# Hybrid decoder block on one core: the hi and lo halves of q and k carried across the partitions by DMAs instead of by 64-row copies, with a scheduler that models drains

## The chip, the cores and the metric

The kernel runs on one core of one Trainium2 chip. The metric is the device time of one execution in microseconds (us). The kernel before takes 1377.05 us (median of 3 runs, 1376.73 to 1377.36). TensorE (PE) does matrix products, VectorE (DVE) and ScalarE (ACT) do elementwise work, GpSimd (POOL) clears a few buffers, and SyncE (SP) issues every DMA from one queue, in the order in which the program lists them. Each engine works through its own list in order; between engines, semaphores make an instruction wait for what it reads, and for the buffer that it overwrites.

## What is computed

The reference is a decoder trunk of two layers over one sequence of 512 tokens, model width 1024, in float32. Cut to what matters here, a layer is:

```
h = rmsnorm(x, norm_g);  proj = h @ w_in
# branch A: differential attention, 8 heads, 2 maps of 64
q = rope(rmsnorm(aq)); k = rope(rmsnorm(ak))
a = softmax(causal(q0 k0^T)) - lam * softmax(causal(q1 k1^T))
oa = rmsnorm(a @ av) * silu(az);  ya = oa @ w_out_a
# branch B: mLSTM matrix memory, 8 heads, q and k of 64 columns
mq, mk = split(silu(causal_conv(bqk)))
hb = rmsnorm(mlstm(mq, mk, bv, bi, bf)) * sigmoid(bo) * silu(bz);  yb = hb @ w_out_b
u = sigmoid(ga) * ya + sigmoid(gb) * yb
x = x + u @ w_o
```

## The kernel before, in words

**Precision in two halves.** Matrix products run in float32r, a reduced form of float32. To keep accuracy, an operand is kept as two tiles: hi, the value cast to float32r (an ACT copy), and lo, the rest (a DVE subtraction); `split` at line 453 records the pair. A product of two such operands is three matmuls: hi by hi, hi by lo, lo by hi (`mm3`, line 457). So each weight piece of 128x1024 is loaded into one of two raw buffers (`wr`), cast into `wh`, and subtracted into `wl`; `wh` and `wl` have three buffers each. With `wsp` set, the subtraction is done in two halves of 128x512 (line 1388).

**Pieces.** A layer is 104 weight pieces and a small one for the gates. The order of the named groups stands in `TUNE["order"]`: `qk0` are the four pieces that make q and k of heads 0 and 1 (chunk c = 0 of 4), `av` the values, `az`, `ga`, `gb`, `bo`, `bz` the gates, `bqk` q and k of branch B, `woa`, `wob`, `wo` the output products.

**q and k of branch A.** When a chunk's product for 128 tokens (tt = 0 to 3) is complete, `qk_done` (line 744) makes the squares for the norm and the rotary turn. Then `back` (line 809) lets PE transpose four 128x128 blocks into one PSUM tile `qkt`. That tile comes from a pool with a single buffer (tag `tr`), which also serves `ut` (the transposed attention weights), `msp`, `den`, `gft` and others, so the next of these can't start until the last reader of the previous one is done. In `qkt`, rows 0 to 63 hold map 0 and rows 64 to 127 map 1. The score product of each map wants q as hi in one 64-row half and lo in the other, and k as hi in both. So `back` reads `qkt` ten times in pieces of 64x256: six ACT copies (q hi, k hi twice, for each map) and four DVE subtractions (q lo, k lo, for each map), half of them crossing from one half of the partitions to the other. There are 32 such backs in a run: 2 layers, 4 chunks, 4 blocks of tokens.

**q and k of branch B.** `bqk_done` (line 917) does the same after the convolution: for each of 8 pieces in a layer, ACT copies and DVE subtractions of 64x512 out of the tile `cv`.

**The order of the work.** Engines' lists are not written by hand. All operations are first recorded with their dependences (`Recorder.add`, line 159), then `schedule` (line 252) plays them through a model of five engines: at each step the engine that can start first takes, of what is ready, the operation with the least key (a due time worked back from the matmul that needs it). SP takes the earliest recorded. The costs, latencies and due times in `TUNE` set the order; the chip then runs the lists as they are, and waits where the model was wrong.

**Tiles named below.** `s2` is a ring of seven 128x512 buffers for short-lived tiles. Tiles `qk_0x` and `qk_2x`, or `qs` and `ks`, hold q and k of a chunk for the score products `sc`; `kl` holds k lo. `mq`, `mql` and `mk` are their like in branch B. `dd` and `em` are decay tables of branch B, read by DMAs from a DRAM tile `rows`.

Of the kernel before, what the change touches and what calls it, by code (L numbers as in the profile page):

```python
# [9 lines left out]
F32 = mybir.dt.float32  # L10
# [27 lines left out]
    "order": (  # L38
# [4 lines left out]
    ),  # L43
    "qkt": 4,
    "gct": 14,
    "gls": 6,
    "glf": 10,
    "attn": (1, 5, 5, 9, 9, 10, 13, 16, 16, 19, 24),
    "a0": 23,
    "ap": 18,  # L50
    "a4": 6,
    "ml": (0, 10, 11, 12, 16, 28),
    "ahead": 3,
    "lc": 2,
    "slack": 3400.0,
    "margin": 200.0,
    "pemargin": 0.0,
    "wait": 300.0,
    "swpen": 6000.0,
    "smargin": 135.0,  # L60
    "pwait": 7.0,
    "wdiff": 8000.0,
    "wsp": 1,
    "kact": (0, 1, 2),
    "qsq": (1, 3),
    "foldA": (0, 2, 3, 4, 5, 6, 7),
    "foldM": (0, 1, 2, 3, 4, 5, 6, 7),
    "foldD": (0, 1, 2, 3, 4, 5, 6, 7),
    "warm": 18,
    "start": 'x0 ng w0 x1 ct w1 x2 x3',  # L70
    "gateA": 10,
    "gateM": 4,
    "actp": (0, 3),
    "m0": 221,
    "mp": 14,
    "m4": 10,
    "slots": 20,
}

# [17 lines left out]
class Recorder:  # L97
# [61 lines left out]
    def add(self, eng, e, fn, a, k):  # L159
# [41 lines left out]
        if eng == "PE":  # L201
            self.pe_time += cost
        self.ops.append({"eng": eng, "e": e, "fn": fn, "a": a, "k": k, "pre": preds, "cost": cost, "nom": self.pe_time})

    @staticmethod
    def cost(eng, fn, a, k):
# [25 lines left out]
        if eng == "DVE":  # L232
# [13 lines left out]
            return x  # L246
        return 60.0

# [3 lines left out]
    def schedule(self):  # L252
# [32 lines left out]
        for i in reversed(range(n)):  # L285
            o = ops[i]
            v = o["nom"] if o["eng"] == "PE" else o["nom"] + TUNE["slack"]
# [11 lines left out]
        table = 6  # L299
        order = []  # L300

        def admit(i):
# [11 lines left out]

        todo = [i for i in range(n) if not left[i]]
        while len(order) < n:
            for i in todo:
                ready[ops[i]["eng"]].append(i)
            todo = []
            best = None  # L320
            cand = {}
            for e, r in ready.items():
                c = []
                for i in r:
                    s = admit(i)
                    if s is not None:
                        c.append((s, i))
                if c:
                    cand[e] = c
# [17 lines left out]
            ready[e].remove(i)  # L347
            s = max(s, pick[2])
            load = None
            o = ops[i]  # L350
            c = o["cost"]
            if e == "ACT":
                sets = self.ACT_SET.get(self.func(o))
                if sets and table not in sets:
                    s = max(s, free[e] + 1283.0)
                    table = sets[0]
                    load = table
            free[e] = s + c
            end[i] = s + c
            if e == "SP":  # L360
                size = 4.0
                for x in list(o["a"][0].shape):
                    size *= x
                dma = max(dma, s) + size / 360.0
                end[i] = max(dma, s) + 2000.0
            for t in o["tiles"]:
                r = rings[t["ring"]]
                if not t["live"]:
                    t["live"] = True
                    m = min(r["free"])  # L370
                    r["free"].remove(m)
# [5 lines left out]
                if not t["left"]:  # L377
                    r["free"].append((t["rel"], t["name"]))
            o["load"] = load
            order.append((s, len(order), i))  # L380
# [28 lines left out]
def kernel(ctx, tc, x, pos, wp, wg, cst, par, pb, ngb, out):  # L409
# [181 lines left out]
    def layer_events(l):  # L591
# [208 lines left out]
        def qk_back(c, tt, rq):  # L800
# [8 lines left out]
            def back():  # L809
# [3 lines left out]
                ts = slice(tt * P, (tt + 1) * P)  # L813
                q0, q1, k0, k1 = (t[:, :, ts] for t in st[("qs", c)])
                kl0, kl1 = (t[:, :, ts] for t in st[("kl", c)])
# [101 lines left out]
        def bqk_done(m, acc):  # L917
# [17 lines left out]
            if kind == 0:  # L935
# [432 lines left out]
    def prep(i):  # L1368
# [131 lines left out]
```

## Time and profile before

| | before |
|---|---|
| median of 3 runs | 1377.05 us |
| profiled execution, device time | 1378.8 us |
| its span (first to last instruction) | 1377.0 us |
| PE busy | 1354.3 us (98%) |
| DVE busy | 999.8 us (73%) |
| ACT busy | 883.7 us (64%) |
| DMA queue of SP | 48304 packets, 136.54 MB, 33.0% of 16 engines |

How to read it: busy is time in which an engine has an instruction in flight. Matmuls are pipelined, so the records of two neighbours overlap, and a busy PE may still be short of its full rate. A group's row in the profile names the line, the engine, the operation, the tile written and the tiles read, the shape, the count, the busy time, the mean of one in ns, and the engine's idle time just before them, with what ended it. Every operation of this kernel has the same line (405 before, 429 after), because the recorder issues them all; so tiles tell the operations apart.

### The profile page before, as it was taken

How to read it: one execution, taken by the hardware profiler on the slowest of the kernel's cores; microseconds unless marked ns; L12 is line 12 of the kernel's file. 1: busy time of each engine (PE TensorE's matmuls, PEld its weight loads, DVE VectorE, ACT ScalarE, POOL GpSimd, SP SyncE). 2: the span in 40 equal slices, each digit the busy share in tenths (PEclk: the TensorE clock that was granted, in tenths of full speed). 3: DMA queues.
4: the chain of work that ended last, by engine and by line, in shares of the span. 5: the costliest groups of instructions: out<-in, count | busy, mean ns of one | idle time of the engine just before them, and what ended most of it. 6: DMA issues, size and time to landing. Idle time of an engine off the chain costs nothing.

```text
span 1377.0 us, 17949 instructions
## 1 busy us (share of the span) xinstructions
PE 1354.3 (98%) x6356; PEld 1099.4 (80%) x6356; DVE 999.8 (73%) x1974; ACT 883.7 (64%) x1808; POOL 23.0 (2%) x28
## 2 busy tenths in 40 slices
PE   9999999999999999999999999999999999999999
PEld 7787777888888878888887877878788877888887
DVE  7988988886367868844569889888853777787442
ACT  6868968886246858733366788688752467687230
POOL 1000010000000000000000000000000000000000
PEclk9999999999999999999999999999999999999999
DMA  4222221223334444433512222221333444444332
GB/s 174 92 63 92 62 78 62 77 77 111 95 108 127 119 117 124 131 102 108 189 49 92 63 75 77 78 71 53 116 90 103 108 125 120 117 119 129 104 119 86
DMA packets 48394, 137.68 MB, mean 100 GB/s; under 512 B 5776, under 2 KB 12560, under 8 KB 48304
## 3 DMA queue, kind: packets, MB, share of 16 engines
q1 hardware_dynamic: 48304, 136.54, 33.0%
q8 instruction: 50, 0.82, 0.2%
q14 instruction: 40, 0.33, 0.1%
HBM read 132.25 MB, written 4.26 MB: 99 GB/s over the span
## 4 chain that ended last, share of the span: by engine, by line
PE 63%; DVE 15%; ACT 14%; DMA 5%; issue 2%; SPq 1%; ACTq 0%; DVEq 0%
PE qk L405 10%; PE wo L405 6%; PE wob L405 6%; PE bv L405 6%; PE woa L405 6%; PE gb L405 5%; PE av L405 4%; PE bo L405 4%; DVE wl L405 3%; DMA dd<-rows 3%; PE bz L405 3%; PE ga L405 3%; PE bqk L405 3%; ACT wh L405 2%; ACT p L405 2%
## 5 line engine op out<-in xcount | busy, mean ns | idle before, releaser
L405 DVE TENSOR_TENSOR wl<-wr,wh 128x512 fp32r<-128x512 f32 x400 | 265.7, 686 | 103.9 <-ACT wh L405 100.0
L405 ACT CAST wh<-wr 128x1024 fp32r<-128x1024 f32 (+1 forms) x202 | 210.9, 1044 | 201.7 <-PE woa L405 43.8
L405 PE MATMUL qk<-wh,hh 128*128 128x512 f32 x256 | 99.5, 405 | 0.2 <-ACT hh L405 0.2
L405 PE MATMUL qk<-wh,hl 128*128 128x512 f32 x256 | 99.4, 401 | 0.0
L405 PE MATMUL qk<-wl,hh 128*128 128x512 f32 x256 | 98.9, 402 | 0.1
L405 ACT ACTIVATE p<-sc,mx,rq 128x128 f32<-128x128 f32 (+3 forms) x128 | 78.8, 618 | 12.8 <-DVE mx L405 12.2
L405 PE MATMUL wob<-ob,wh 128*128 128x512 f32 x256 | 84.7, 389 | 0.0
L405 PE MATMUL woa<-oa,wh 128*128 128x512 f32 x256 | 79.9, 389 | 0.0
L404 ACT ACT_TABLE_LOAD x61 | 78.3, 1283 | 1.1
L405 PEld LDWEIGHTS qk<-wl,hh 128*128 128x128 f32 x256 | 48.0, 188 | 11.1 <-DVE wl L405 2.1
L405 PEld LDWEIGHTS wob<-ob,wh 128*128 128x128 f32 x256 | 48.0, 188 | 10.1
L405 PEld LDWEIGHTS woa<-oa,wh 128*128 128x128 f32 x256 | 48.1, 188 | 9.8
L405 PEld LDWEIGHTS qk<-wh,hh 128*128 128x128 f32 x256 | 48.1, 188 | 9.6 <-ACT hh L405 0.5
L405 PEld LDWEIGHTS qk<-wh,hl 128*128 128x128 f32 x256 | 48.1, 188 | 9.1 <-DVE hl L405 0.4
L405 DVE TENSOR_REDUCE mx<-sc 128x2 f32<-128x256 f32 (+1 forms) x64 | 52.5, 820 | 0.7
L405 PE MATMUL az<-hh,wh 128*128 128x512 f32 x128 | 50.5, 402 | 0.0
L405 PE MATMUL bo<-hl,wh 128*128 128x512 f32 x128 | 50.3, 393 | 0.0
L405 PE MATMUL bo<-hh,wh 128*128 128x512 f32 x128 | 50.3, 393 | 0.0
L405 PE MATMUL bo<-hh,wl 128*128 128x512 f32 x128 | 50.3, 393 | 0.0
L405 PE MATMUL az<-hl,wh 128*128 128x512 f32 x128 | 50.2, 400 | 0.0
L405 PE MATMUL az<-hh,wl 128*128 128x512 f32 x128 | 49.3, 395 | 0.0
L405 PE MATMUL bqk<-hh,wl 128*128 128x512 f32 x128 | 48.2, 397 | 0.7 <-DVE wl L405 0.7
(273 smaller groups left out, 3661.4 us busy)
## 6 DMA issues: line engine op xcount, KB each, us to landing
wr<-in_wp_dram SPq DMA_DIRECT2D x208, 512.0 KB, 3.5
dd<-rows SPq DMA_DIRECT2D x16, 256.0 KB, 4.0
em<-rows SPq DMA_DIRECT2D x16, 256.0 KB, 3.4
dd<-rows SPq DMA_DIRECT2D x16, 192.0 KB, 5.1
x<-in_x_dram SPq DMA_DIRECT2D x4, 512.0 KB, 7.4
dd<-rows SPq DMA_DIRECT2D x16, 128.0 KB, 6.2
xr<-in_x_dram SPq DMA_DIRECT2D x8, 256.0 KB, 4.3
x1d<-xn SPq DMA_DIRECT2D x8, 256.0 KB, 3.6
```

The source lines that it names most:

```text
L404: self.tc.keep_in_program_order(self.nc.scalar.preload_act_table_set(self.SET_NAME[o["load"]]))
L405: self.tc.keep_in_program_order(getattr(o["e"], o["fn"])(*o["a"], **o["k"]))
```

## The change

Three things change.

First, `back` and `bqk_done` no longer copy in 64-row pieces. A new helper `halves` takes two `s2` tiles and makes hi and lo of the whole 128x512 tile, one ACT copy and one DVE subtraction. Then DMAs, issued by SP, carry each 64-row half to its places, ten of 64x256 (64 KB) for each back, six or four of 64x512 (128 KB) for each piece of branch B. That is 320 and 80 DMAs more in a run.

Second, the scheduler's model. A DMA's issue costs 400 ns instead of 60, a transfer that doesn't come from the DRAM inputs goes at 175 bytes per ns instead of 360, and an ACT or DVE instruction whose first output or input starts at another partition than that of the instruction before it starts 115 ns later (and is put off by `drain` in the choice). There are also a bias on the due time by the kind of tile, and a penalty for starting late.

Third, the table. The order of pieces and the offsets are new, `ahead` is 5 instead of 3, `wsp` is 0, so that `wl` is one subtraction of 128x1024. Some small choices move: `qsq` and `kact` let ACT do fewer column-wise squares and scalings, `actp` one block more, and `foldM` and `foldD` lose one head each, which adds four matmuls.

```
     "order": (
...
-    "wsp": 1,
-    "kact": (0, 1, 2),
-    "qsq": (1, 3),
+    "wsp": 0,
+    "kact": (0, 1),
+    "qsq": (1,),
...
-        return 60.0
+        return 400.0
...
+                    if e in at_rows and ops[i]["rows"] != at_rows[e]:
+                        k += TUNE["drain"]
+                    if s - q < TUNE["risk"] and e != "SP":
+                        k += TUNE["late"]
...
+            if e in at_rows:
+                if o["rows"] != at_rows[e]:
+                    s = max(s, free[e] + 115.0)
+                at_rows[e] = o["rows"]
...
-                dma = max(dma, s) + size / 360.0
+                src = o["a"][1]
+                dma = max(dma, s) + size / (175.0 if src.space != DRAM or src.tensor.name.startswith("rows") else 360.0)
...
+    def halves(src, name):
+
+        hi, lo = t2(f"h_{name}", F32R), t2(f"l_{name}", F32R)
+        split(hi, lo, src)
+        return hi.bitcast(F32), lo.bitcast(F32)
...
+                h4, l4 = halves(pst.rearrange("p a b -> p (a b)"), f"qk{l}_{c}_{tt}")
+                h4, l4 = (t.rearrange("p (a b) -> p a b", a=4) for t in (h4, l4))
...
                 for q, k, kl, a, b in ((q0, k0, kl0, L, H), (q1, k1, kl1, H, L)):
-                    A.copy(q[a], pst[a, 0:2, :])
-                    V.tensor_tensor(q[b], pst[a, 0:2, :], q[a].bitcast(F32), ALU.subtract)
-                    A.copy(k[a], pst[a, 2:4, :])
-                    A.copy(k[b], pst[a, 2:4, :])
-                    V.tensor_tensor(kl[a], pst[a, 2:4, :], k[a].bitcast(F32), ALU.subtract)
+                    SY.dma_start(q[a], h4[a, 0:2])
+                    SY.dma_start(k[a], h4[a, 2:4])
+                    SY.dma_start(k[b], h4[a, 2:4])
+                    SY.dma_start(q[b], l4[a, 0:2])
+                    SY.dma_start(kl[a], l4[a, 2:4])
...
+            hi, lo = halves(y, f"m{l}_{m}")
...
-                    A.copy(q[a, i, :], y[a])
-                    A.copy(q[b, i, :], y[a])
-                    V.tensor_tensor(st[("mql", grp)][i][a, pl, :], y[a], q[a, i, :].bitcast(F32), ALU.subtract)
+                    SY.dma_start(q[a, i, :].bitcast(F32), hi[a])
+                    SY.dma_start(q[b, i, :].bitcast(F32), hi[a])
+                    SY.dma_start(st[("mql", grp)][i][a, pl, :].bitcast(F32), lo[a])
...
-                    A.copy(k[a, i, :], y[a])
-                    V.tensor_tensor(k[b, i, :], y[a], k[a, i, :].bitcast(F32), ALU.subtract)
+                    SY.dma_start(k[a, i, :].bitcast(F32), hi[a])
+                    SY.dma_start(k[b, i, :].bitcast(F32), lo[a])
...
-        if TUNE["wsp"]:
+        if i < TUNE["wsp"]:
```

How the lists move is shown at two places. The first is DVE's list in layer 0, while the last chunk (c = 3) is turned: tile `qkt0_3_0` is its first block of tokens, `qs` and `kl` the q and k lo of that chunk, `wl30` a weight's lo. Before:

```order
L405 TENSOR_TENSOR qs00_3_497<-qkt0_3_0_533,qs00_3_497 64x2x128
L405 TENSOR_TENSOR rq0_3_503<-qy0_3_1_509,qt0_3_1_510 128x16
L405 TENSOR_TENSOR wl30_489<-wr30_487,wh30_488 128x512 x2
L405 TENSOR_REDUCE qss0_3_2_516<-sq0_3_2_515 128x8
L405 TENSOR_TENSOR rot0_3_2_517<-qk0_3_2_469,ctab0_143 128x512
L405 TENSOR_TENSOR kl00_3_501<-qkt0_3_0_533,ks00_3_499 64x2x128
L405 TENSOR_TENSOR sq0_3_2_515<-qk0_3_2_469,stab0_144 128x8x32 x2
L405 TENSOR_TENSOR qs10_3_498<-qkt0_3_0_533,qs10_3_498 64x2x128
L405 TENSOR_TENSOR rot0_3_2_517<-rot0_3_2_517,sq0_3_2_515 128x512
L405 TENSOR_TENSOR sc0_5_0_529<-sc0_5_0_529,ct_94 128x2x128
L405 TENSOR_TENSOR kl10_3_502<-qkt0_3_0_533,ks10_3_500 64x2x128
```

After, the same place of DVE's list:

```order
L429 TENSOR_TENSOR rot0_3_3_535<-qk0_3_3_488,ctab0_154 128x512
L429 TENSOR_TENSOR l_qk0_3_0_548<-qkt0_3_0_546,h_qk0_3_0_547 128x512
L429 TENSOR_TENSOR sq0_3_3_534<-qk0_3_3_488,stab0_155 128x8x32 x2
L429 SCALAR_TENSOR_TENSOR mx0_4_3_543<-mx0_4_3_543,rq0_2_396 128x2
L429 RECIPROCAL sums0_4_2_524<-sums0_4_2_524 128x2
L429 TENSOR_TENSOR rot0_3_3_535<-rot0_3_3_535,sq0_3_3_534 128x512
L429 TENSOR_TENSOR sums0_4_2_524<-sums0_4_2_524,ml0_158 128x2
L429 TENSOR_TENSOR wl31_500<-wr31_498,wh31_499 128x1024
```

Four reads of the PSUM tile with nine other instructions between them have become one read.

The second place is SP's list in layer 0, around the load of piece 9 (`wr9`, the first of `qk1`). Before, the loads follow each other:

```order
L405 DMA wr5_154<-in_wp_dram 128x1024
L405 DMA wr6_175<-in_wp_dram 128x1024
L405 DMA wr7_185<-in_wp_dram 128x1024
L405 DMA wr8_192<-in_wp_dram 128x1024
L405 DMA wr9_201<-in_wp_dram 128x1024
L405 DMA wr10_211<-in_wp_dram 128x1024
```

After, with the q and k of chunk 0 in `qk0_0x` (`h_qk0_0_3` and `l_qk0_0_3` are the new hi and lo tiles of its last block of tokens):

```order
L429 DMA kl10_0_165<-l_qk0_0_2_195 64x2x128
L429 DMA qk0_0x_163<-h_qk0_0_3_197 64x2x128 x3
L429 DMA qk0_0x_163<-l_qk0_0_3_198 64x2x128
L429 DMA kl00_0_164<-l_qk0_0_3_198 64x2x128
L429 DMA qk0_0x_163<-h_qk0_0_3_197 64x2x128 x3
L429 DMA qk0_0x_163<-l_qk0_0_3_198 64x2x128
L429 DMA kl10_0_165<-l_qk0_0_3_198 64x2x128
L429 DMA wr9_199<-in_wp_dram 128x1024
L429 DMA wr10_206<-in_wp_dram 128x1024
```

These are the last of forty DMAs of chunk 0 that now stand between `wr7` and `wr9`, with `wr8` alone among them. On PE's list the first matmul that reads the weights of `wr9` stands 127 matmuls after the last transpose of `qkt0_0_0`, the block whose halves the forty DMAs begin with: 89 of 512 columns, 4 of 384, 5 of 256 and 29 of 128 or fewer. In layer 1 the load after chunk 0's first twenty is `wr114`, and that after all forty is `wr115`.

More of the change, by code (lines that the diff above doesn't have):

```diff
@@ L45 @@
     "gct": 14,
-    "gls": 6,
-    "glf": 10,
-    "attn": (1, 5, 5, 9, 9, 10, 13, 16, 16, 19, 24),
+    "gls": 7,
+    "glf": 12,
+    "attn": (1, 5, 5, 9, 9, 10, 13, 16, 16, 19, 26),
     "a0": 23,
     "ap": 18,
[L51 to L55, printed above, removed]
-    "margin": 200.0,
[L57 to L62, printed above, removed]
-    "wsp": 1,
-    "kact": (0, 1, 2),
@@ L65 @@
-    "qsq": (1, 3),
+    "a4": 8,
+    "ml": (2, 8, 10, 10, 15, 30),
+    "ahead": 5,
+    "lc": 10,
+    "slack": 11872.4,
+    "margin": 200.0,
+    "pemargin": 560.8,
+    "wait": 223.4,
+    "swpen": 7168.1,
+    "smargin": 15.0,
+    "pwait": 0.5,
+    "wdiff": 2579.7,
+    "wsp": 0,
+    "kact": (0, 1),
+    "qsq": (1,),
     "foldA": (0, 2, 3, 4, 5, 6, 7),
-    "foldM": (0, 1, 2, 3, 4, 5, 6, 7),
-    "foldD": (0, 1, 2, 3, 4, 5, 6, 7),
+    "foldM": (0, 1, 2, 3, 4, 5, 6),
+    "foldD": (0, 1, 2, 3, 4, 5, 7),
@@ L69 @@
     "warm": 18,
     "start": 'x0 ng w0 x1 ct w1 x2 x3',
[L71 to L76, printed above, removed]
+    "gateA": 9,
+    "gateM": 0,
+    "actp": (0, 1, 3),
+    "m0": 226,
+    "mp": 15,
+    "m4": 7,
     "slots": 20,
+    "bias": {'ga': -5500.0, 'sgb': -13300.0, 'den': -10150.0, 'bo': 2250.0, 'qk': -150.0, 'bv': -10450.0, 'gft': 3750.0, 'az': 1250.0, 'bqk': 1600.0, 'ut': 11800.0, 'ht': -10800.0, 'ct': 3400.0, 'wo': -4600.0, 'mk': 15900.0, 'sums': -3350.0, 'num': 10200.0, 'av': -250.0, 'qk0_0x': -5500.0, 'qk1_0x': -2750.0, 'gm': -4750.0, 'sq': -4250.0, 'ang': -4950.0, 'warm': -3250.0, 'ms_a': -3050.0, 'woh': 2250.0, 'mq': -1100.0, 'junk': -5800.0, 'ob': -9500.0, 'glf': -11200.0, 'fb_b': 200.0, 'gct': 2700.0, 'l_m': -850.0, 'ua': -450.0, 'rnh': -1350.0, 'qk0_2x': 4600.0, 'rot': 7600.0, 'pb': 4950.0, 'ss': -1350.0, 'ul': 4100.0, 'qt': -450.0, 'wol': 650.0, 'gi': -2850.0, 'fo_b': -800.0, 'gt': 800.0, 'msl_b': 4800.0, 'kl': -2350.0, 'gc': 350.0, 'gw': 1950.0, 'msl_a': 2900.0, 'fb_d': -1250.0, 'taz': 1400.0, 'cv': -1200.0, 'par': 3250.0, 'hl': -900.0, 'x': -1200.0, 'msh_d': 4200.0, 'sbz': -100.0, 'msh_a': 1300.0, 'x1d': 650.0, 'stab': 600.0, 'ctab': -1750.0, 'sbo': 10700.0, 'tbz': -250.0, 'posf': -7500.0, 'ones': -7500.0, 'hh': -450.0, 'sc': -50.0, 'qss': 200.0, 'zeroc': -150.0, 'msp_b': 1300.0, 'msh_b': 3500.0, 'l_qk': -150.0, 'mql': -1050.0, 'eps': 2500.0, 'sdh': -900.0, 'qy': 4250.0, 'ml': -6450.0, 'fb_a': 2750.0, 'posi': 200.0, 'fo_a': -950.0, 'msl_d': -150.0, 'rq': -100.0, 'rows': 200.0, 'bz': 100.0},
@@ L78 @@
+    "drain": 2306.5,
+    "risk": 209.6,
+    "late": 392.0,
 }
@@ L202, in add @@
             self.pe_time += cost
-        self.ops.append({"eng": eng, "e": e, "fn": fn, "a": a, "k": k, "pre": preds, "cost": cost, "nom": self.pe_time})
+        rows = None
+        if eng in ("ACT", "DVE"):
+            rows = tuple(x.offset // math.prod(list(x.tensor.shape)[1:]) for x in [a[0]] + ins[:1])
+        self.ops.append({"eng": eng, "e": e, "fn": fn, "a": a, "k": k, "pre": preds, "cost": cost, "nom": self.pe_time, "rows": rows, "kind": a[0].tensor.name.rstrip("_0123456789")})
     @staticmethod
@@ L286, in schedule @@
             o = ops[i]
[L287 removed]
+            v = o["nom"] + TUNE["bias"].get(o["kind"], 0.0) + (0.0 if o["eng"] == "PE" else TUNE["slack"])
             for j in succ[i]:
@@ L300, in schedule @@
         order = []
+        at_rows = {"ACT": (0, 0), "DVE": (0, 0)}
         def admit(i):
@@ L318, in schedule @@
                 ready[ops[i]["eng"]].append(i)
+                cand[ops[i]["eng"]] = None
             todo = []
             best = None
[L321 to L327, printed above, removed]
+            for e in engs:
+                c = cand[e]
+                if c is None:
+                    c = []
+                    for i in ready[e]:
+                        s = admit(i)
+                        if s is not None:
+                            c.append((s, i))
+                    cand[e] = c
                 if c:
-                    cand[e] = c
                     s = max(free[e], min(c)[0])
@@ L347, in schedule @@
             ready[e].remove(i)
+            cand[e] = None
             s = max(s, pick[2])
```

7 lines of the change are left out of this document (5 added, 2 removed), and 8 rows, old and new, of the table TUNE.

## The prediction

> **What bounds the kernel now.** I read the page first, then TensorE by stretches, then the waits in front of TensorE, then single waits in the timeline, and last the groups of ScalarE, VectorE and the DMAs.
>
> ```profile
> span 1377.0 us, 17949 instructions
> PE 1354.3 (98%) x6356; PEld 1099.4 (80%) x6356; DVE 999.8 (73%) x1974; ACT 883.7 (64%) x1808; POOL 23.0 (2%) x28
> PEclk9999999999999999999999999999999999999999
> ```
>
> TensorE (PE) is busy for 98% of the span, at a full granted clock throughout. Two stretches from the table by stage (busy us of PE, PEld, DVE, ACT and POOL with counts, then clock, DMA share, GB/s) and one piece of the chain that ended last (start, length) show how:
>
> ```profile
> 148.00:197.00 49.00, 47.57 (x240) 38.27 (x239) 42.52 (x100) 41.36 (x107) 3.79 (x4) 1.00 0.27 82
> 344.00:393.00 49.00, 49.00 (x217) 40.55 (x216) 16.87 (x27) 11.57 (x13) 0.00 (x0) 1.00 0.32 97
> 337.38 18.81 PE woa L405 x83
> ```
>
> From 344 us on, PE is never idle, and VectorE (DVE) and ScalarE (ACT) have 17 and 12 us of work in 49. There 83 matmuls took 18.81 us, so a matmul of 512 columns costs 226.6 ns, and 217 of them fill the 49 us. In the attention stage, 148 to 197 us, DVE and ACT are busy for 87% and 84%, and PE loses time. The change takes no matmul away, so all that it can win is PE's waiting: 1377.0 - 1354.3 = 22.7 us of idle time, its start and end among it, and the refilling of the pipeline after each wait. The waits of PE (total us, times, longest):
>
> ```profile
> PE den L405 <- DVE fo_d L405: 2.9, 4, 1.4
> PE qkt L405 <- DVE kl L405: 2.6, 8, 0.5
> PE ut L405 <- DVE kl L405: 2.2, 6, 0.5
> PE warm L405 <- DVE ml L405: 1.6, 1, 1.6
> PE qkt L405 <- ACT qs L405: 1.5, 2, 0.8
> PE ht L405 <- DMA ct<-in_cst_dram: 1.4, 1, 1.4
> PE ut L405 <- DVE ul L405: 1.3, 2, 0.8
> PE qkt L405 <- ACT qk_2x L405: 0.9, 2, 0.5
> PE num L405 <- DVE ms_b L405: 0.8, 2, 0.4
> PE bqk L405 <- DVE wl L405: 0.7, 1, 0.7
> PE sc L405 <- ACT p L405: 0.6, 2, 0.3
> PE av L405 <- ACT qk_0x L405: 0.5, 2, 0.2
> PE av L405 <- DVE sq L405: 0.3, 1, 0.3
> PE qk L405 <- ACT hh L405: 0.2, 1, 0.2
> PE gft L405 <- DVE kl L405: 0.2, 1, 0.2
> ```
>
> Five rows are waits for the one PSUM buffer of the transposes, until the 64-row copies of q and k have read it: qkt for kl, qs and qk_2x, ut for kl, gft for kl. Together they are 2.6 + 1.5 + 0.9 + 2.2 + 0.2 = 7.4 us in 19 waits. The other rows, without the two of the start (warm, ht), are 7.3 us in 15. What a wait costs beyond its idle time stands in the timeline of that stretch (start, length; idle time before in brackets):
>
> ```profile
> 225.71 0.63 PE L405 MATMUL qkt<-ct,rot 128*128 128x128 f32 x4 [0.40 <-DVE kl L405]
> 228.51 0.41 DVE L405 TENSOR_TENSOR kl<-qkt,ks 64x256 fp32r<-64x256 f32 x1
> 231.51 0.43 DVE L405 TENSOR_TENSOR kl<-qkt,ks 64x256 fp32r<-64x256 f32 x1
> 232.57 0.40 PE L405 MATMUL az<-hh,wl 128*128 128x512 f32 x1
> 233.73 0.33 PE L405 MATMUL qkt<-ct,rot 128*128 128x128 f32 x1 [0.76 <-ACT qs L405]
> ```
>
> From the end of az (232.97) to that of qkt (234.06) are 1.09 us. Four transposes take 0.63 us and one 0.33, so each further one is 0.10. Lost are 1.09 - 0.10 = 0.99 us for 0.76 of idle time: 0.23 on top of each wait. So the 19 waits cost 7.4 + 19 x 0.23 = 11.8 us, and the 15 others 7.3 + 15 x 0.23 = 10.8. The first three rows show the cause: the buffer was written at 226.34 and read until 231.94, for 5.6 us, since its small reads stand in two full queues.
>
> **The change part by part.** The price of the elementwise work, before and after (count, busy us, mean ns of one):
>
> ```profile
> L405 ACT CAST ks<-qkt 64x256 fp32r<-64x256 f32 x64 | 23.5, 367 | 3.9 <-DVE qs L405 2.0 <-PE qkt L405 1.0
> L405 ACT CAST mq<-cv 64x512 fp32r<-64x512 f32 x32 | 19.8, 619 | 1.4 <-DVE cv L405 0.9
> L405 ACT CAST bv<-bv 128x512 fp32r<-128x512 f32 x16 | 9.4, 586 | 21.1 <-PE bv L405 21.1
> L405 DVE TENSOR_TENSOR kl<-qkt,ks 64x256 fp32r<-64x256 f32 x32 | 13.4, 419 | 1.5 <-ACT ks L405 0.9
> L405 DVE TENSOR_TENSOR mk<-cv,mk 64x512 fp32r<-64x512 f32 x16 | 11.0, 686 | 0.5
> L405 DVE TENSOR_TENSOR ul<-ut,uh 128x512 fp32r<-128x512 f32 x16 | 11.0, 687 | 1.7 <-ACT uh L405 1.5
> L405 DVE TENSOR_TENSOR wl<-wr,wh 128x512 fp32r<-128x512 f32 x400 | 265.7, 686 | 103.9 <-ACT wh L405 100.0
> L405 DVE TENSOR_TENSOR wol<-wr,woh 128x1024 fp32r<-128x1024 f32 x8 | 9.8, 1225 | 13.8 <-ACT woh L405 13.7
> ```
>
> An instruction over 64 rows costs as much as one over 128, so whole tiles are cheap. Branch A: six ACT copies at 367 ns become one at about 586 (the bv row has its shape and source), 32 times: 32 x (2.20 - 0.59) = 51.5 us of ACT. Four DVE subtractions at 419 become one at 687 (the ul row): 32 x (1.68 - 0.69) = 31.7 us of DVE. Branch B: 48 ACT copies and 32 DVE subtractions at 0.62 and 0.69 become 16 each: 19.8 and 11.0 us. The weights' lo in one instruction: 200 x (2 x 0.686 - 1.225) = 29.4 us of DVE. So ACT gives up some 71 us of 884 and DVE some 72 of 1000. The small choices (squares, scalings, folds) move tens of instructions from ACT to DVE and back; I set them at nothing, since both engines idle for over a quarter of the span, and if that cover is gone they are part of the second term's bounds.
>
> None of these 143 us is on the path itself; they count where PE waits. First term: after the change the transpose buffer is held for 0.59 + 0.69 and two handovers, about 1.5 us instead of 5.6. I let the 11.8 us shrink in that ratio, to 3.2: a gain of 8.6 us. Its bounds are 11.8, if all such waits go, and nothing, if the copy stands just as long in ACT's queue. Second term: the other 10.8 us, for which a shorter queue on DVE and the new order both work. I take 3, a quarter of it, since the largest of them (den behind fo_d, num behind ms_b) lie in branch B, where little is taken off. Bounds are the 10.8 gained, and as much lost if the new order waits elsewhere. Third term: four matmuls more, 4 x 0.227 = 0.9 us lost.
>
> Fourth term: the DMAs. 320 transfers of 64 KB and 80 of 128 KB join SP's one queue. The rows that bear on them (DMA issues by kind with KB and median us from issue to landing; four issues in a row; the queue's packets, MB and share):
>
> ```profile
> wr<-in_wp_dram SPq DMA_DIRECT2D x208, 512.0 KB, 3.5
> dd<-rows SPq DMA_DIRECT2D x16, 128.0 KB, 6.2
> dd<-rows SPq DMA_DIRECT2D x16, 64.0 KB, 7.0
> out_dram<-xr SPq DMA_DIRECT2D x2, 128.0 KB, 1.7
> 473.49 1.81 SPq L405 DMA_DIRECT2D dd<-rows  x4
> q1 hardware_dynamic: 48304, 136.54, 33.0%
> ```
>
> Issues follow at 1.81 / 4 = 0.45 us. No row shows a transfer from SBUF to SBUF. One out of SBUF (out_dram) lands after 1.7 us, so I take 2.0, and a pace set by the issue, 0.45. The bound above is the chain of dd, read from DRAM: its last 64 KB, issued 0.45 us after the 128 KB, lands 7.0 - 6.2 + 0.45 = 1.25 us behind it. I choose the lower end because the mean packet, 0.33 x 16 x 1377 / 48304 = 0.15 us for 2.8 KB, makes eight packets of 512 bytes on each of 16 engines 0.22 us if the time goes by size.
>
> Who waits for them? In most places nobody: chunks 1 to 3 and branch B are made well ahead of their scores. The tight place is chunk 0, whose 40 DMAs stand in front of the load `wr9` in layer 0. Count from the last transpose of its first block: the copy, 0.8 us with its handover; 41 issues, 18.5; the load, 3.5; the cast of the weight, 1.05; its lo, 1.23; two handovers, 0.4: wl is there at 25.5. PE gets there after 89 matmuls of 512 columns, 20.2 us, 9 of 384 or 256, 1.2, and 29 small ones, 2.9: 24.3, and wants wl one matmul later, at 24.5. That is 1.0 us lost. In layer 1 the loads stand between the DMAs with over 8 us to spare. The first scores of layer 1 come after 24 matmuls of 512 columns and 6 transposes, at 6.0 us, and want six DMAs: 0.8 + 2.7 + 2.0 = 5.5, or 7.0 with the 3.5 us of a load. For these, for the same in layer 0, and for the two `s2` buffers that each back now holds until its DMAs have landed (other work queues behind an ACT copy that waits for one), I charge 1.0 us in all.
>
> **The sum:** -8.6 - 3.0 + 0.9 + 1.0 + 1.0 = -8.7 us. The profiled execution took 1378.8 us, 1.8 more than its span, and 1.75 more than the median of the runs. So the same execution would take 1370.1, and the median 1377.05 - 8.7 = 1368.4.
>
> **The rivals.** (1) The DMAs are paced by their transfers, not by their issue. At a pace of p us, `wr9` comes 41 x (p - 0.45) + 1.0 late in layer 0. In layer 1 the fourth score block, 26.8 us of matmuls behind the same transpose, waits for all of chunk 0, 0.8 + 41p + 2.0, so for 41p - 24.0 where that is positive. Against it stand 8.6 + 3.0 - 0.9 = 10.7 us, so it decides from p = 0.64 on. At 0.7 the two cost 11.3 + 4.7, and the median is 1382.4; at 1.25, the bound of dd, 33.8 + 27.3, and it is 1427. For it speaks the dd chain; against it the 1.7 us of out_dram.
>
> The Trainium skill has a rule that points this way ("DMA: Bandwidth & Descriptors", section "Bandwidth"): transfers under 64 KB are dominated by their descriptors, and its table has 0.95 us for 64 KB, at 138 GB/s, a load from DRAM on another issuing path. As an estimate, 0.95 as the pace would cost 21.5 + 15.0 us and put the median at 1403. The dd rows agree with its direction (1.25 us), and no run here yet shows it for SBUF to SBUF.
>
> (2) The buffer's waits come back in other forms: ACT and DVE are still full in the attention stage, the copy comes late in their lists, and one subtraction of 1.2 us delays short instructions behind it. Half of the first term and none of the second: -4.3 + 0.9 + 2.0 = -1.4, or 1375.7, no change to the eye (a measurement of this kernel tells 0.2%, or 2.75 us, from none). For it speaks that DVE is 87% busy there now, and gives up only a fourteenth of its work.
>
> (3) The new order removes nearly all waits and the DMAs cost nothing: -11.8 - 10.8 + 0.9 = -21.7, or 1355.4. For it speaks that the waits are short and regular in both layers; against it that den and num are chains of their own.
>
> **How the numbers follow.** The forecast, a gain of 3 to 17 us, gets 0.54; (3) gets 0.10; (2) gets 0.12; (1) gets 0.15 for a pace up to 0.8 and 0.09 above. So faster is 0.64, the same 0.12, slower 0.24. The range starts at 1356, near (3), and ends at 1390, where (1) stands at a pace of 0.8 (41 x 0.35 + 1.0 + 8.8 = 24.2 lost against 10.7 won); about half of (3) and the heavy part of (1) are left out.
>
> **What would show it.** Right: PE's waits for kl, qs and qk_2x are gone or under 3 us, the copy h_qk takes near 0.59 us and l_qk near 0.69, ACT and DVE are some 70 us less busy each, and SP's issues of q and k stand 0.45 us apart and land after 2 to 2.5. Wrong: sc or qk wait for DMAs by several us at the start of a layer, or the landing times of q and k grow along the forty, as those of dd do. If the waits for the buffer are gone and the time has not fallen, look for new waits at ut, den and num, and for ACT waiting for `s2` buffers.

## The result: slower by 1.6%, and the profile after

The changed kernel took 1398.54 us (median of 4 runs, 1396.77 to 1402.14), the kernel before 1377.2 us beside it (4 runs, 1376.73 to 1377.48). The ratio is 1.0159, with a 95% interval from 1.0135 to 1.0182. The forecast was 1368.4 us, a gain, in a range that ended at 1390. The profiled execution took 1396.94 us. Its page:

```profile
span 1395.2 us, 18219 instructions
PE 1351.6 (97%) x6360; PEld 1115.1 (80%) x6360; DVE 942.2 (68%) x1658; ACT 806.1 (58%) x1481; POOL 23.2 (2%) x28
q1 hardware_dynamic: 100784, 168.02, 42.0%
```

ACT is 883.7 - 806.1 = 77.6 us less busy and DVE 57.6 us less, where the prediction had 71 and 72. PE's idle time has not fallen but nearly doubled: 1395.2 - 1351.6 = 43.6 us, where it was 22.7. The table by stage says where (us, busy us of PE, PEld, DVE, ACT and POOL with counts, clock, DMA share, GB/s):

```profile
49.00:98.00 49.00, 39.43 (x188) 31.26 (x187) 28.64 (x69) 20.52 (x46) 0.00 (x0) 0.93 0.41 112
148.00:197.00 49.00, 47.92 (x239) 38.40 (x237) 39.92 (x84) 32.24 (x80) 2.00 (x2) 1.00 0.37 97
197.00:246.00 49.00, 43.57 (x205) 36.46 (x206) 35.44 (x77) 29.37 (x75) 0.00 (x0) 0.93 0.36 106
344.00:393.00 49.00, 49.00 (x218) 40.58 (x217) 20.40 (x23) 16.34 (x20) 0.00 (x0) 1.00 0.33 98
```

The middle of the layer (344 us) is as full as before. The stretch at 148 us is a little better than before (47.92 us of PE against 47.57), with less work on DVE and ACT. The loss is in two places of each layer, here 49 to 98 and 197 to 246 us, and there the granted clock is 0.93, where the kernel before has 1.00 in every such stretch; the page, in slices of 35 us, prints 9 tenths throughout. PE's waits (total us, times, longest):

```profile
PE qk L429 <- DVE av L429: 11.6, 2, 5.9
PE av L429 <- ACT uh L429: 5.9, 1, 5.9
PE av L429 <- ACT av L429: 4.4, 1, 4.4
...
PE gft L429 <- DVE l_qk L429: 2.9, 2, 1.9
PE sc L429 <- DMA qk_0x<-l_qk: 2.5, 4, 1.1
PE qkt L429 <- DVE l_qk L429: 2.1, 3, 1.6
...
PE ut L429 <- DVE l_qk L429: 0.8, 2, 0.4
```

The waits for kl, qs and qk_2x are gone. The first three rows are new: four stops, 11.6 + 5.9 + 4.4 = 21.9 us. The releasers that they name, av and uh, are not to blame, as the timeline around the first stop shows. SP's list ends the forty copies of chunk 0 (start, length):

```profile
70.11 0.59 SPq L429 DMA_DIRECT2D kl<-l_qk  x1
70.75 8.32 SPq L429 DMA_DIRECT2D wr<-in_wp_dram  x4
```

Only then, at 70.75 us, is `wr9` issued. ACT, DVE and PE in the same stretch (idle time before an instruction in brackets):

```profile
69.80 0.39 PE L429 MATMUL av<-wh,hh 128*128 128x512 f32 x1
...
74.71 1.04 ACT L429 CAST wh<-wr 128x1024 fp32r<-128x1024 f32 x1 [7.79 <-DMA wr<-in_wp_dram]
75.66 0.36 ACT L429 CAST uh<-ut 128x256 fp32r<-128x256 f32 x1
75.79 1.23 DVE L429 TENSOR_TENSOR wl<-wr,wh 128x1024 fp32r<-128x1024 f32 x1 [7.67 <-ACT wh L429]
76.08 0.58 PE L429 MATMUL av<-uh,av 128*128 128x256 f32 x1 [5.89 <-ACT uh L429]
...
80.35 0.63 PE L429 MATMUL qk<-wh,hl 128*128 128x512 f32 x1
80.78 0.61 PE L429 MATMUL qk<-wh,hh 128*128 128x512 f32 x1
```

ACT stood 7.79 us before the cast of `wr9`, and DVE 7.67 before its lo. Behind these two, in lists that are worked in order, stood uh and the work that PE needed. So one late load stopped all three engines, and the row of PE names only the last link. PE did not even get as far as the matmul that reads `wr9`: it stopped at 70.2 us for uh, which stands behind the cast of `wr9` in ACT's list. After the stop the matmuls follow each other at 80.78 - 80.35 = 0.43 us instead of 0.227: the granted clock is at half there, from 74.4 to 81.2 us. In the table of stretches the column next to the DMA share has it:

```profile
74.50:81.10 6.60, 4.28 (x13) 3.25 (x14) 5.17 (x9) 5.51 (x11) 0.00 (x0) 0.50 0.49 163
```

The second stop has the same cause at chunk 2. The chain of waits of that stretch runs through SP's issues, one behind the other, into the load:

```profile
194.55 0.60 SPq L429
195.19 0.61 SPq L429
195.84 3.60 DMA wr<-in_wp_dram
199.47 1.05 ACT wh L429
200.55 1.22 DVE wl L429
...
202.43 1.65 PE qk L429 x3
```

The issues of the copies start 0.65 us apart, where I had taken 0.45. The tile kl by itself (durations in ns, least, median and most), and the landing of the copies (KB, median us from issue):

```profile
L429 SPq DMA_DIRECT2D kl<-l_qk x64: 590/605/1289, 47.1 to 951.1; - x64
```

```profile
kl<-l_qk SPq DMA_DIRECT2D x64, 64.0 KB, 2.0
qk_0x<-h_qk SPq DMA_DIRECT2D x48, 64.0 KB, 2.0
```

They land after 2.0 us, as taken (medians), and this does not grow along the forty: those at the end of both layers' forty take 2.0 as well. The transfers are not slow. It is SP that needs 0.605 us for the issue of such a copy, and 0.65 from one to the next, against 0.33 for a load of weights. Why such a copy takes longer to issue is not shown.

### The profile page after: what moved, and what is told of

It reads as the page before. It is cut to its first block, busy times and chain, and to the rows that moved or that the text cites. A ratio compares the mean times of both kernels' runs of the same rounds, so it can differ in the third digit from the quotient of the medians.

```text
span 1395.2 us, 18219 instructions
## 1 busy us (share of the span) xinstructions
PE 1351.6 (97%) x6360; PEld 1115.1 (80%) x6360; DVE 942.2 (68%) x1658; ACT 806.1 (58%) x1481; POOL 23.2 (2%) x28
## 2 busy tenths in 40 slices
DMA packets 100875, 169.18 MB, mean 121 GB/s; under 512 B 12176, under 2 KB 59920, under 8 KB 100784
## 3 DMA queue, kind: packets, MB, share of 16 engines
q1 hardware_dynamic: 100784, 168.02, 42.0%
## 4 chain that ended last, share of the span: by engine, by line
PE 76%; DVE 8%; DMA 5%; SPq 5%; ACT 4%; issue 2%; DVEq 0%; ACTq 0%
PE qk L429 11%; PE bv L429 6%; PE wo L429 6%; PE wob L429 6%; PE woa L429 6%; PE bqk L429 6%; PE ga L429 6%; PE gb L429 5%; PE bz L429 5%; SPq L429 5%; PE bo L429 5%; PE az L429 3%; PE sc L429 2%; DMA dd<-rows 2%; PE av L429 2%
## 5 line engine op out<-in xcount | busy, mean ns | idle before, releaser
L429 DVE TENSOR_TENSOR wl<-wr,wh 128x1024 fp32r<-128x1024 f32 x200 | 244.0, 1221 | 150.0 <-ACT wh L429 147.3
L429 PE MATMUL qk<-wh,hh 128*128 128x512 f32 x256 | 95.7, 407 | 12.1 <-DVE av L429 11.6
L429 PE MATMUL qk<-wh,hl 128*128 128x512 f32 x256 | 96.0, 403 | 0.0
L429 PE MATMUL woa<-oa,wh 128*128 128x512 f32 x256 | 86.6, 390 | 0.0
L429 PEld LDWEIGHTS wob<-ob,wh 128*128 128x128 f32 x256 | 47.6, 188 | 10.7
L429 PE MATMUL av<-uh,av 128*128 128x256 f32 x192 | 45.6, 285 | 10.5 <-ACT uh L429 5.9
L429 PE MATMUL bqk<-hh,wh 128*128 128x512 f32 x128 | 50.8, 397 | 0.0
L429 PE MATMUL bqk<-hl,wh 128*128 128x512 f32 x128 | 50.4, 394 | 0.0
```

Source lines behind the costliest of these rows:

```text
L429: self.tc.keep_in_program_order(getattr(o["e"], o["fn"])(*o["a"], **o["k"]))
```

## The experiments

Theory A: SP's pace of 0.65 us an issue costs the time, since what stands behind the copies in its one list (weight loads, later copies) comes late. Against it stood B, that the transfers between partitions themselves, or their load on the DMA engines, cost it; and C, that the new order of the other engines costs it. Where an expectation names only one rival, it is the one that the run can tell from A. All ratios are to the kernel before, run beside on the same chip (1377.4 to 1377.6 us).

**1. The weight loads moved ahead of the copies.** Only SP's list differs: a load goes ahead of copies as soon as all that read its raw buffer's last tile has been issued.

```
-        order = self.schedule()
+        order = self.hoist(self.schedule())
...
+            if o["eng"] == "SP" and o["a"][1].tensor.name[:2] in ("h_", "l_"):
+                while nxt < len(loads) and nxt > 7 and not left[nxt - 2]:
+                    out.append(loads[nxt])
...
```

> Only SP's list changes: a weight load that stands behind DMAs of q and k moves ahead of them, as far back as the point where the raw buffer it fills has been read. All other engines' lists are those of the changed kernel. Theory A (each of those DMAs takes 0.65 us of SP, so the loads behind forty of them come late, TensorE stops four times for 4.4 to 5.9 us, and its clock is halved for a while after each stop): the four stops with the slow matmuls behind them are about 31 us, so 1362 to 1372 us. Theory B (the new order of the work is itself worse): 1390 us or more. Theory C (q and k land late, and the score products or the ACT copies wait for that): no better than 1390 us, since q and k now come later still.

Measured: 1378.68 us, ratio 1.001 (1.0001 to 1.0019). 19.9 of the 21.3 us lost come back, and the four long stops are gone. But the time is not the 1362 to 1372 that A expected. PE's waits now:

```profile
PE ut L457 <- DVE l_qk L457: 5.3, 2, 2.9
...
PE sc L457 <- DMA kl<-l_qk: 2.9, 1, 2.9
PE qkt L457 <- DVE l_qk L457: 2.7, 3, 1.1
PE gft L457 <- DVE l_qk L457: 2.6, 1, 2.6
PE sc L457 <- DMA qk_0x<-l_qk: 2.2, 3, 1.5
```

PE waits 15.7 us for l_qk and for copies. Why l_qk is late, DVE's own row shows:

```profile
173.12 0.69 DVE L457 TENSOR_TENSOR l_qk<-qkt,h_qk 128x512 fp32r<-128x512 f32 x1 [2.96 <-DMA kl<-l_qk]
```

It stood 2.96 us until a copy of an earlier tile had read the `s2` buffer that it writes. So the pace acts in a second way: each back holds two of the seven `s2` buffers until its ten copies are issued and done, and the transpose's PSUM buffer waits behind that. I refined A: late loads are one part, late copies that hold buffers the other.

**2. The true price in the scheduler.** The model's DMA issue costs 650 ns instead of 400, nothing else.

```
-        return 400.0
+        return 650.0
```

> The scheduler's price of a DMA issue is 650 ns instead of 400, nothing else; it makes new lists for all engines. Theory A: it now sees how long SP is taken up, puts the loads ahead by itself or the matmuls behind them later, and the long stops go: 1360 to 1380 us. Theory B: 1385 us or more, since table and rules are the same.

Measured: 1380.95 us, ratio 1.0029 (1.0017 to 1.0041), 1 us above the band that A named. The plan itself, given the right price, avoids most of the loss; stops of up to 2.5 us stay, at sc behind p and at qk behind wh.

**3. The new order without the copies.** The table and scheduler of the change, with the old 64-row instructions in place of `halves` and the DMAs.

```
-                    SY.dma_start(q[a], h4[a, 0:2])
...
+                    A.copy(q[a], pst[a, 0:2, :])
...
```

> The table and the scheduler of the changed kernel, with the ten 64-row copies of q and k as before and no DMA for them. Theory A: no long stops, and the waits for the transpose buffer are back (about 12 us): 1365 to 1382 us. Theory B: the order is to blame, so 1388 us or more.

Measured: 1395.89 us, ratio 1.0134 (1.0117 to 1.015): the rival's number. There is no copy there, and the time is almost that of the change, by other stops (DVE is at 991.8 us again):

```profile
PE av L429 <- DVE sq L429: 5.3, 3, 2.3
```

So the new table and scheduler, planned for the old instructions, are a loss of 18.5 us. By this run alone C could have been the whole cause.

**4. The copies in the old order.** The kernel before, its table and scheduler kept (a DMA issue at 60 ns), with the halves by DMAs on SP.

> The DMAs of the halves alone: table and scheduler of the kernel before, which prices a DMA issue at 60 ns. Theory A: the model thinks that forty DMAs take SP 2.4 us where they take 26, so loads and scores come later by up to 20 us for each chunk: 1410 to 1470 us. Theory B: the order of before is good and the DMAs do no harm: 1365 to 1380 us.

Measured: 1457.31 us, ratio 1.0589 (1.0563 to 1.0616). In an order that takes an issue for nearly free, the copies cost 80 us, inside A's band.

**5. Two queues.** The decisive run. All lists are those of the change, but six of the ten copies of a back, those that fill k, are issued by GpSimd (2% busy) instead of SP. The copies and their bytes, the order and the other engines' work stay.

```
+    SG = rec.engine("SP", nc.gpsimd)
...
-                    SY.dma_start(k[a], h4[a, 2:4])
-                    SY.dma_start(k[b], h4[a, 2:4])
+                    SG.dma_start(k[a], h4[a, 2:4])
+                    SG.dma_start(k[b], h4[a, 2:4])
...
-                    SY.dma_start(kl[a], l4[a, 2:4])
+                    SG.dma_start(kl[a], l4[a, 2:4])
```

> The changed kernel, with the six copies of a tile that fill k (k[a], k[b] and kl[a] of both heads) issued by GpSimd instead of SyncE; every engine's list in the same order otherwise, the weight loads where the change has them. Theory A (SyncE's issue pace of 0.65 us makes the weight loads behind the copies late): SyncE issues 16 instead of 40 copies at the start of a layer, so the load behind them starts some 15 us earlier, the four stops of 4 to 6 us at TensorE go, and the time falls to 1362-1382 us, if GpSimd's issue takes no more than about 1.1 us (6 x 1.1 is as long as 10 x 0.65). Theory B (the copies themselves or the new order of the other engines cost the time): 1390 us or more. If GpSimd's issue takes 1.5 us and over, the copies come later than from one queue: the wait of VectorE's l_qk for a buffer that a copy still reads grows, and the time stays over 1390 us with the weight loads in time.

Measured: 1356.86 us (1354.98 to 1359.08), ratio 0.9848 (0.9834 to 0.9863), 5 us below the band of A. The page, its stages, SP's list where `wr9` stands, and PE's waits:

```profile
span 1356.8 us, 18309 instructions
PE 1342.9 (99%) x6360; PEld 1112.7 (82%) x6360; DVE 942.2 (69%) x1658; ACT 805.9 (59%) x1481; POOL 134.4 (10%) x220
```

```profile
49.00:98.00 49.00, 48.48 (x245) 39.84 (x245) 39.72 (x93) 28.68 (x77) 10.95 (x18) 1.00 0.49 129
```

```profile
57.80 21.81 SPq L429 DMA_DIRECT2D wr<-in_wp_dram  x6
```

```profile
PE den L429 <- DVE ms_b L429: 4.1, 2, 2.1
...
PE sc L429 <- DMA qk_0x<-l_qk: 0.7, 2, 0.5
...
PE qkt L429 <- DVE l_qk L429: 0.2, 1, 0.2
```

`wr9` is issued at 57.80 us instead of 70.75; the stretch from 49 us on has 48.48 us of PE work, not 39.43; and l_qk makes PE wait 0.2 us in all. GpSimd takes as long for an issue as SP, and its copies land later than those of the change, as do those that SP still issues (2.5 to 4.6 us by tile). GpSimd's issue in ns, then KB and median us to landing:

```profile
L429 POOL DMA_DIRECT2D kl<-l_qk x64: 585/592/597, 45.3 to 904.0; - x64
```

```profile
kl<-l_qk POOLq DMA_DIRECT2D x64, 64.0 KB, 3.0
qk_0x<-h_qk POOLq DMA_DIRECT2D x32, 64.0 KB, 3.8
```

One thing beside the issuing engine differs, the packets (queue, packets, MB, share of 16 engines):

```profile
q1 hardware_dynamic: 73136, 155.42, 39.6%
q0 software_dynamic: 6144, 12.60, 3.8%
```

GpSimd's 192 copies are 6144 / 192 = 32 packets each, where SP makes (100784 - 73136) / 192 = 144 of one. But all packets together take 43.4% of the DMA engines' time, not less than the 42.0% of the change. B falls: the same copies with the same bytes, landing later and loading the DMA engines no less, cost nothing that shows. C falls as the cause by itself too, since the order is the same. That the count of packets does not decide either, run 9 shows.

**6. Two queues, and the loads moved ahead as well** (runs 5 and 1 together).

> The run before this one with the weight loads moved ahead of the copies as well. It tells apart the two ways in which the issue pace costs time: the late weight load, and the late copies (kl, qk_0x) with the buffers of h_qk and l_qk that they hold. Theory A with both parts: the first run with the weight loads moved (all copies on SyncE) kept stops of 14 us where l_qk waited for its buffer or scores for a copy; with 16 copies on SyncE these fall to under 5 us, and the time to 1362-1374 us. If only the weight loads counted, the time is that of the run without this move, within 3 us, and the l_qk waits are as many as there.

Measured: 1364.64 us (1358.62 to 1367.23), ratio 0.9902 (0.987 to 0.9933). In the band that was named, but above run 5: where the loads are no longer late, moving them ahead delays the copies, as I read PE's waits (3.3 + 1.5 us for l_qk, and 2.0 for qk_0x).

**7. Fewer issues, the same bytes.** Run 1, with the hi parts of q and k of one head carried by one DMA of 128 KB in chunks 0 and 2. For this the edit also lays q and k of a head side by side in the chunk's tile.

```
-                    st[("qs", c)] = [xt[:, 2 * i : 2 * i + 2, :] for i in range(4)]
+                    st[("xt", c)] = xt
+                    st[("qs", c)] = [xt[:, 2 * i : 2 * i + 2, :] for i in (0, 2, 1, 3)]
...
+                    if c % 2 == 0:
+                        SY.dma_start(st[("xt", c)][a, 4 * r : 4 * r + 4, ts].bitcast(F32), h4[a])
...
```

> The weight loads moved ahead, and for chunks 0 and 2 the copies of the hi part of q and of k of one head into the same 64 partitions joined in one DMA of 64x4x128 (the two lie side by side): 8 instead of 10 DMAs for a tile, the same bytes. Theory A (the pace goes by the issue, about 0.6 us each whatever it carries): the joined DMA takes 0.6 us to issue, a tile's copies 5.2 instead of 6.5 us, the waits of l_qk and of the scores fall by 3 to 6 us against the same kernel with 10 copies (1378.7), to 1371-1377 us. If the pace goes by bytes, or by the 64 x 4 rows, the joined DMA takes 0.9 to 1.2 us to issue and the time stays at 1377-1381 us.

Measured: 1374.14 us, ratio 0.9973 (0.9963 to 0.9984), 4.5 us under run 1 and in A's band. The hi copies of chunk 0, half of them now twice as large, take as long to issue as before:

```profile
L457 SPq DMA_DIRECT2D qk_0x<-h_qk x32: 590/608/1140, 43.8 to 740.4; - x32
```

The median of the sixteen joined ones by themselves is 607 ns, that of the others 613. So the pace goes by the issue, not by bytes.

**8. Both remedies on one queue** (runs 1 and 2 together).

> The changed kernel with the scheduler's price of a DMA issue at the measured 650 ns instead of 400, and the weight loads moved ahead in the list that comes out. Theory A: each alone took the time from 1398.5 to 1381 and 1378.7 us; what is left in each is different (stops of 2 to 3 us behind weight loads in the one, l_qk waiting for its buffer in the other), so both together give 1366-1377 us. Theory B (the two only do the same thing): 1377-1382 us.

Measured: 1397.27 us, ratio 1.0141 (1.0125 to 1.0157). Both expectations missed. PE waits 3.7 + 2.9 + 2.5 us at sc for copies, where run 2 had 0.3, and still 4.8 us at sc for p. My reading is that the plan with the right price had already placed the loads, and that moving them again pushes the copies back; which of the moved loads does it was not tried.

**9. All ten copies on GpSimd.** One queue and one pace for the copies, as in the change, but SP has its loads to itself.

> The changed kernel with all ten copies of a tile issued by GpSimd: SyncE's list holds the weight loads alone at the start of a layer, and the copies have the same single pace as in the change (0.59 us an issue on GpSimd, 0.65 on SyncE). It takes away the late weight loads alone and leaves the late copies with the buffers that they hold. Theory A: the four long stops go, the waits of l_qk for its buffer and of scores for a copy stay at 8 to 14 us, the time is 1366-1380 us, between the two-queue run (1356.9) and the change (1398.5). If the late loads were all that mattered, it is 1355-1361 us; if the pace of the copies were all, over 1385.

Measured: 1374.02 us, ratio 0.9966 (0.9954 to 0.9978), in A's band. The long stops are gone, and the waits of the second kind stay:

```profile
PE qkt L429 <- DVE l_qk L429: 3.7, 3, 2.2
PE ut L429 <- DVE l_qk L429: 3.7, 2, 2.0
...
PE sc L429 <- DMA qk_0x<-l_qk: 2.0, 1, 2.0
```

This splits the 41.7 us between the change and run 5: 1398.5 - 1374.0 = 24.5 us for the late loads, 1374.0 - 1356.9 = 17.1 for the late copies. The split is rough: GpSimd's issues start 0.58 us apart, not 0.65, and run 1, which frees the loads and delays the copies, won 19.9. With 54704 + 10240 packets on the two queues this run has fewer than run 5 and is slower, so it is not the count of packets that made run 5 fast.

**10. Chunk 2 alone back on one queue.** Run 5, with chunk 2's copies all on SP.

```
+                KQ = SY if c == 2 else SG
...
```

> The two-queue run with the copies of chunk 2 (of both layers) all back on SyncE, chunks 0, 1 and 3 left on two queues. It prices the part that the prediction left out: the load behind the 24 copies of chunk 2. Theory A: a stop of 5 to 6 us near 190 to 200 us and one in layer 1, each with slow matmuls after it worth 2 to 3 us, and l_qk's buffer waits of 1 to 3 us in each layer: 1356.9 + 17 to 23 = 1373-1380 us. If only the loads of chunk 0 mattered, as the prediction had it, under 1361 us.

Measured: 1378.27 us (1375.69 to 1381.0), ratio 1.0003 (0.9994 to 1.0012): 21.4 us more than run 5, half of the 41.7 and in A's band, for a part that the prediction had not counted. The wait is the change's, 11.6 us in two stops, with half clock behind each of the two:

```profile
PE qk L429 <- DVE av L429: 11.6, 2, 6.2
```

**11. The old order with two queues** (run 4, with k's copies on GpSimd).

> The halves by DMAs in the order of the kernel before (its table and its scheduler, a DMA issue priced at 60 ns), which took 1457.3 us with all copies on SyncE; here the k copies are issued by GpSimd. Theory A (the issue pace is what makes the copies dear): most of the 80 us go, 1365-1395 us; below 1377.4 the halves alone would be a gain without the new table. If the new order is what the halves need, it stays over 1410.

Measured: 1407.43 us, ratio 1.0217 (1.02 to 1.0235). Of the 80 us of run 4, 50 go; that is less than A expected, and 30 stay. In the old order, even with two queues, l_qk stands behind copies that hold its buffer, and PE behind l_qk:

```profile
PE qkt L405 <- DVE l_qk L405: 13.0, 4, 3.9
```

**12. Branch B's copies on GpSimd too:** on top of run 5, 48 of its 80 copies (one of mq's two, mql, and the lo of mk; the 112 of the expectation is a miscount).

> The two-queue run with the second copy of mq, the copies of mql and the lo copy of mk (branch B, 112 copies in all) issued by GpSimd as well. Theory A: there is little left behind those copies, since TensorE waits for ms_b and not for mq or mk; 1354-1358 us, no difference from 1356.9 that can be told. If GpSimd's issues there come behind its memsets, or weight loads had been held by them, up to 4 us either way.

Measured: 1355.77 us (1354.63 to 1362.4), ratio 0.9853 (0.9833 to 0.9873). No difference from run 5 that can be told.

## Why the prediction was wrong

**The relief was right in kind.** ACT fell by 77.6 us (forecast 71), DVE by 57.6 (72); of the 14.4 us by which DVE fell short, 7.7 are the weights' lo, which went from 265.7 us to 244.0, a fall of 21.7 and not of 29.4. The whole-tile instructions took what was taken for them (0.582 and 0.686 us, against 0.59 and 0.69):

```profile
L429 DVE TENSOR_TENSOR l_qk<-qkt,h_qk 128x512 fp32r<-128x512 f32 x32 | 21.9, 686 | 13.5 <-DMA qk_0x<-h_qk 6.2 <-ACT wh L429 2.3 <-ACT p L429 2.0
L429 ACT CAST h_qk<-qkt 128x512 fp32r<-128x512 f32 x32 | 18.6, 582 | 22.3 <-PE qkt L429 20.3 <-DMA qk_0x<-h_qk 0.8 <-DMA ks<-h_qk 0.5
```

**The first and second terms** were right in direction and too small. Run 5, where PE waits only 0.9 us for l_qk and for copies, shows what relief and order are worth: its span is 20.2 us shorter than that of before, near the third rival's 21.7. The forecast had 8.6 + 3.0. Of the 20.2 us, 8.8 are idle time of PE (22.7 to 13.9) and 11.4 its busy time (1354.3 to 1342.9, with four matmuls more); the working had 34 waits x 0.23 = 7.8 us of busy time at most, and what else went there is open. In the change as it is, less of it shows, since l_qk still waits for the buffer that it writes: PE's waits for l_qk are 2.9 + 2.1 + 0.8 = 5.8 us, not under 3.

**The fourth term is the step that failed,** at three points.

First, the pace. "a pace set by the issue, 0.45" was right in kind, and measured 0.65. I had taken four reads of DRAM for the price of a copy from SBUF to SBUF, which no row showed. The first rival had the price right in numbers, "it decides from p = 0.64 on", and wrong in its cause: the landing stays at 2.0 us. With p = 0.65 its working gives 41 x 0.20 + 1.0 = 9.2 us in layer 0 and 41 x 0.65 - 24.0 = 2.65 in layer 1, against 10.7 won: 1378 us. That is no change, not 1398.5, so the pace is not the whole of it.

Second, the places. "chunks 1 to 3 and branch B are made well ahead of their scores" is true of their scores (PE's rows have 0.2 us at most for one of their tiles, a kl), and overlooks the loads that stand behind their copies. The load behind chunk 2's 24 copies stopped PE for 5.8 us in each layer; run 10 puts 21.4 us on this chunk. That 1378 + 21.4 comes out at 1399 is luck: this sum has 10.7 us won, where run 5 won 20.5, and 11.9 us lost on chunk 0, where 41.7 - 21.4 = 20.3 us are left for it and the rest. Even for chunk 0 the working counted to the matmul that reads `wr9`, and PE had stopped before it, for uh. Also in layer 1, "the loads stand between the DMAs with over 8 us to spare" failed: at 0.65 us, forty issues take 8 us more than at 0.45, and the stop there was 4.4 us.

Third, what a stop costs. I took idle time and 0.23 us. The four stops here are 21.9 us idle, and behind each of them the clock was at half for 6.83 us, with 4.42, 5.11, 4.58 and 4.57 us of matmuls in it, 18.7 in all. At a pitch of 0.43 instead of 0.227 that loses, as an estimate, 18.7 x (1 - 0.227 / 0.43) = 8.8 us. Run 5 has two stretches of 3.41 us at half clock, full of matmuls, which by the same working cost it 3.2.

So the difference between the change and run 5, 1395.2 - 1356.8 = 38.4 us by their spans, can be added up. PE's idle time differs by 43.6 - 13.9 = 29.7 us: 21.9 in the four stops, 5.6 more of waits for l_qk, 1.8 more of sc for its copies. PE's busy time differs by 8.7: 8.8 - 3.2 = 5.6 are the half clock. Some 3 us of busy time stay open.

The Trainium skill has the clock's rule ("TensorE: Matmul & The Clock Gate", Part 1): the clock falls to half after an idle window of about 3.4 us and comes back after a busy one, and the windows run free, 3413 ns each. The trace agrees on the lengths: 6.83 us of half clock, two such windows, go with each of the four stops, all longer than 3.4 us. It does not bear out that a stop must be so long: in run 5 stops of 2.09 and 1.97 us were each followed by 3.41 us of half clock. The rule on small transfers in the Trainium skill ("DMA: Bandwidth & Descriptors", section "Bandwidth"), that they are dominated by their descriptors, is the one from which the prediction had estimated 1403. That this is close to the result is chance, and the runs show another cause: a copy twice as large takes as long to issue (run 7), and with the same copies on two queues the kernel took 1356.9. The sentence that bears on it stands on another page of the Trainium skill ("Trainium Kernel Development and Optimization", Key Constraints): issuing from several engines saves only the sequencer's issue time. Here the second issuing engine was worth 41.7 us.

**The fourth rival that I did not have.** Runs 3 and 11 say that new order and copies need each other: the order without the copies costs 18.5 us, the copies without the order 30 even on two queues, both together on two queues win 20.5. I had set the order's share as a sum of its own; it isn't one. In runs 3 and 11 the scheduler also makes new lists for the operations that it gets, so these are prices of a plan and not of one order. That the order was made for the copies is my reading of these three runs; what in the table does it was not tried.

**The chances.** 0.24 went to slower, for paced transfers alone. A row-based bound on the issue's own price was missing: the issues of before lay between 0.28 and 0.48 us (medians by tile), all from or to DRAM, and the working treated 0.45 as known. A factor of 1.5 on it, put through every list position and not only the first, would have led to the load behind chunk 2, though not to the half clock.

## What to carry to other kernels

Count a DMA by what its issue costs the list that it stands in, and look at each thing behind it, not at who needs the data: one late load stopped ACT, DVE and PE by their in-order lists, and PE's row named the wrong culprit. A price that no row shows (here the issue of a copy from SBUF to SBUF) needs a range, and the range has to go through every place where the price enters. When a queue's issue pace is the limit, try a second issuing engine with time to spare: here it took the change from 1.6% slower to 1.5% faster, while none of the orders tried for SP's one queue (runs 1, 2 and 8) made it faster than the kernel before.

## What the hardware showed beside

- An issue of an SBUF to SBUF copy of 64x256 costs 0.60 us on SP and 0.59 on GpSimd (medians of the change and run 5), and on SP 0.61 with 128 KB in one DMA (run 7); a load of 512 KB costs SP 0.33.
- A 64 KB copy is 144 packets when SP issues it and 32 when GpSimd does (run 5).
- With both engines issuing (run 5), the copies land after 2.4 to 3.8 us from GpSimd and 2.5 to 4.6 from SP, where SP alone has 2.0 in the change (medians by tile). It cost nothing that shows here.
- Half clock came in stretches of 3.41 us and multiples. In the runs of the change and its variants every stop of PE of 3.2 us and longer was followed by one. Of those between 2.0 and 3.1 us most were, and several were not; a few of 1.5 to 2.0 us were as well. In the kernel before, with stops up to 1.4 us, there was none.
